# A hybrid decoder block on one core: mixers of two blocks taken together, w_in of the second pair as seven block products, the second MLP product accumulated over all of K

## The chip, the core and the metric

The kernel runs on one core of a Trainium2 chip. The metric is device time in microseconds of one execution; lower is better. The engines named here: PE (TensorE, matmuls), ACT (ScalarE), DVE (VectorE), POOL (GpSimd), SP (SyncE, which issues DMAs).

## What is computed

One layer on x of 2048 rows and 1024 columns, in float32. Cut to what matters:

```python
h = rmsnorm(x, norm_mix_g)
u = h @ w_in                                  # 1024 x 3584
gate_b, gate_c, v, x_r, g = split(u)          # 512, 512, 512, 1024, 1024
y_conv = gate_b * causal_dwconv(gate_c * v, conv_w)
xr = causal_dwconv(x_r, rnn_conv_w) + rnn_conv_b
y_rnn = rg_lru(xr, w_a, b_a, w_x, b_x, lru_lambda) * gelu(g)
y = concat[rmsnorm(y_conv), rmsnorm(y_rnn)]
x = x + y @ w_out                             # 1536 x 1024
z = square(relu(rmsnorm(x, norm_mlp_g) @ w_mlp_in))   # 1024 x 4096
x = x + z @ w_mlp_out                         # 4096 x 1024
out = rmsnorm(x, final_norm_g)
```

`rg_lru` takes two gates r and i from block-diagonal products of xr, forms a = exp(-8 r softplus(-lambda)) and runs the recurrence s = a s + sqrt(1 - a^2) i xr along the rows.

## The kernel before

The 2048 rows are four blocks of 512 (`TB`). Every product is made in three passes: an operand is split into a rounded part (`_hi`, a cast on ACT, L153) and the rest (`_lo`, a subtraction on DVE, L154), and PE multiplies hi by hi, hi by lo and lo by hi. Names ending in these are the two parts.

Blocks are taken in pairs. For a pair b, b + 1 the order is: `mixers(b)` (L933), `w_out_rows(b)` (L958) and `w_out_conv(b)` (L980), `mixers(b + 1)`, `w_out_rows(b + 1)`, `w_out_conv(b + 1)`, then the MLP of both blocks.

- `mixers`: w_in in 14 units of 256 columns, 48 matmuls of 512 columns each (`mm_cols`, L193; tiles ps_x, ps_g, ps_c, ps_v, ps_b). Each weight is loaded and split again for every block. Four units of x_r and g feed four steps of the recurrence (`lru_conv`, `lru_gelu`, `lru_scan`; two channel tiles of 512 rows each; psri are the gate products, L584, and L610 is the scan). Units c, v and b then make the short convolution.
- `w_out_rows` and `w_out_conv` split y (`split_y`, L500 on ACT and L501 on DVE: y_hi, y_lo), multiply by w_out (po, L213), add to x (L970, L993), normalize (L338, tiles xs), and transpose on PE (tps, L976; copied on ACT by L978).
- The first MLP product, `Up` (L675), takes the two blocks as a 2 x 2 block product in seven products (Winograd's form): the operands H1 to H7 are sums of the two blocks' h, the weights sums of four quarters of a slice of w_mlp_in, 8 slices x 7 x 24 matmuls (up, L731). z goes to DRAM (d_z).
- The second, `Down` (L787), does the same with w_mlp_out: four slices `s` of K, in each seven products over two parts `a`, 24 matmuls each (dn, L845); after each product of each slice the sum in PSUM is added to x on DVE (`drain`, L857): 112 additions in all. The weight sums (L815 to L822) are made again for each pair.
- `finish` normalizes the rows and stores them (L874).

What sets the order: inside `manual_schedule` (L400 for the start, L1081 for the MLP, PE only) the instructions stand as written. Elsewhere a scheduler sets the order of each engine's instructions; engines take them strictly in that order, and so does SP's queue of DMAs. Pools of fixed size set how far ahead a load or a split can run (`TSLOTS`, `WSLOTS`).

Of the kernel before, what the change touches and what calls it, by code (L numbers as in the profile page):

```python
# [27 lines left out]
TSLOTS = 29  # L28
WSLOTS = 15
WARM = 6  # L30
AHEAD = 2
# [3 lines left out]
LEAD2 = 2  # L35
ORDER = (1, 2, 6, 5, 7, 3, 4)

ROWS = [
    ("conv_w", 12),
# [11 lines left out]
def block_kernel(  # L51
# [3 lines left out]
    norm_mix_g,  # L55
    w_in,
    conv_w,
    rnn_conv_w,
    rnn_conv_b,
    w_a,  # L60
    b_a,
    w_x,
    b_x,
    lru_lambda,
    g_norm_conv,
    g_norm_rnn,
# [5 lines left out]
    x_t,  # L72
    out,
# [14 lines left out]
    xp = ctx.enter_context(tc.tile_pool(name="xp", bufs=2))  # L88
# [11 lines left out]
    def wtile(name, shape, dt=F32):  # L100
        return wp.tile(list(shape), dt, tag="w", name=name)
# [4 lines left out]
    def wide(name, extra):  # L106
        return xp.tile([P, 2, TB + extra], F32, tag="x", name=name)
# [3 lines left out]


    def src_col(w, col):
        v = w[:, col : col + 256].rearrange("(k p) c -> p k c", p=P)
        return [v[:, 0:4, :], v[:, 4:8, :]], (P, 4, 256)

    def src_row(w, row):
        v = w[row : row + 256, :].rearrange("(j p) n -> p j n", p=P)
        return [v[:, 0:1, :], v[:, 1:2, :]], (P, 1, D)

    def src_quad(w, row):
        v = w[row : row + 512, :].rearrange("(h j p) n -> p h j n", p=P, j=2)
        return [
            v[:, i, :, 512 * c : 512 * c + 512] for i in range(2) for c in range(2)
        ], (P, 2, 512)

    units = []
    for b in range(NB):
        for pr in range(4):
            units.append(("x%d" % pr, src_col(w_in, COL_X + 256 * pr)))  # L130
            units.append(("g%d" % pr, src_col(w_in, COL_G + 256 * pr)))
        for pr in range(2):
            for nm, col in (("c", COL_C), ("v", COL_V), ("b", COL_B)):
                units.append((nm + str(pr), src_col(w_in, col + 256 * pr)))
        for pr in range(4):
            units.append(("oB%d" % pr, src_row(w_out, 512 + 256 * pr)))
        for pr in range(2):
            units.append(("oA%d" % pr, src_row(w_out, 256 * pr)))

    raws = {}  # L140
    splits = {}
    cursor = [0]

    def load_tiles(srcs, shape, name, new):
        tiles = []
        for s in srcs:
            r = new(name, shape)
            nc.sync.dma_start(r, s)
            tiles.append(r)
        return tiles  # L150
# [1069 lines left out]
```

## Time and profile before

| | |
|---|---|
| median of 3 runs | 2210.51 us (2209.82 to 2211.15) |
| span of the profiled execution | 2208.7 us |
| mean granted PE clock | 0.994 |
| matmuls start at full rate at | 28.95 us |
| first pair: mixers and w_out until | 494 us |
| its first MLP product until | 808 us |
| its second MLP product until | 1113 us |
| second pair, last matmul at about | 2183 us |

The profiled execution is one of its own, 1.8 us below the median of the runs; its span is the only time that the profile gives for it. Views used below: the page, the chain of waits, groups of instructions by shape (busy us, mean ns of one, idle time ahead of them and what ended it), windows of time (width, busy us of PE, PEld, DVE, ACT and POOL, granted clock, DMA share, GB/s).

### The profile page before, as it was taken

To read this page: it belongs to the slowest core of one execution; us is meant where nothing else is said; L and a number is where in the kernel's file an instruction comes from. 1 tells how busy PE (TensorE), PEld (TensorE's weight loads), DVE (VectorE), ACT (ScalarE), POOL (GpSimd) and SP (SyncE) were. 2 spreads that over 40 slices of the span, in tenths; PEclk is the share of its full clock that TensorE was granted. 3 is DMA by queue.
4 is the path that set the end of the run, shared out by engine and by line. 5 is a ranking of instruction groups with operands and counts; after the bars stand their busy time and mean duration, and the time that the engine had idled before them with its cause. 6 is when DMAs were issued, how large, how long until landed. Compare 5 with 4: busy or idle time off the path is not lost.

```text
span 2208.7 us, 25232 instructions
## 1 busy us (share of the span) xinstructions
PE 2172.8 (98%) x9684; PEld 1799.6 (81%) x9684; DVE 1670.0 (76%) x1948; ACT 1038.2 (47%) x1346; POOL 62.0 (3%) x62
## 2 busy tenths in 40 slices
PE   7999999999999999999999999999999999999997
PEld 6888888887888888888888888888888888788886
DVE  7787677868775778868888776886796665887867
ACT  4864378534332334334568644764443332433343
POOL 3010000000000000000100000010000000000000
PEclk8999999999999999999999999999999999999999
DMA  7334443432444378454162434233334345854432
GB/s 223 103 123 153 140 155 115 144 116 94 162 152 163 131 254 314 141 177 145 51 234 88 157 120 172 77 115 144 124 114 178 127 166 199 301 207 158 133 103 76
DMA packets 180776, 334.10 MB, mean 151 GB/s; under 512 B 14672, under 2 KB 106928, under 8 KB 180656
## 3 DMA queue, kind: packets, MB, share of 16 engines
q1 hardware_dynamic: 180656, 332.49, 44.0%
q8 instruction: 76, 1.25, 0.2%
q14 instruction: 44, 0.36, 0.1%
HBM read 252.76 MB, written 79.69 MB: 151 GB/s over the span
## 4 chain that ended last, share of the span: by engine, by line
PE 93%; DVE 4%; DMA 1%; SPq 1%; issue 0%; ACT 0%; DVEq 0%
PE dn L845 27%; PE up L731 25%; PE po L213 11%; PE ps_g L193 8%; PE ps_x L193 7%; PE ps_b L193 4%; PE ps_c L193 4%; PE ps_v L193 4%; PE psri L584 2%; DVE H L154 1%; PE start_x L420 1%; PE tps L976 1%; DVE w_lo L154 1%; DVE x L889 0%; DMA z<-d_z 0%
## 5 line engine op out<-in xcount | busy, mean ns | idle before, releaser
L731 PE MATMUL up<-H,w_hi 128*128 128x512 f32 x1792 | 553.7, 390 | 2.6 <-ACT w_hi L153 1.9
L731 PEld LDWEIGHTS up<-H,w_hi 128*128 128x128 f32 x1792 | 336.7, 188 | 73.3 <-ACT w_hi L153 2.7
L731 PE MATMUL up<-H,w_lo 128*128 128x512 f32 x896 | 350.0, 391 | 3.2 <-DVE w_lo L154 3.2
L845 PE MATMUL dn<-w_lo,z_hi 128*128 128x512 f32 x896 | 348.9, 389 | 1.9 <-DVE w_lo L154 1.9
L845 PE MATMUL dn<-w_hi,z_hi 128*128 128x512 f32 x896 | 348.8, 389 | 0.0
L845 PE MATMUL dn<-w_hi,z_lo 128*128 128x512 f32 x896 | 348.8, 389 | 0.0
L153 ACT CAST w_hi<-w 128x1024 fp32r<-128x1024 f32 x156 | 164.1, 1052 | 346.0 <-PE up L731 164.8
L154 DVE TENSOR_TENSOR w_lo<-w,w_hi 128x1024 fp32r<-128x1024 f32 x156 | 190.3, 1221 | 119.6 <-PE up L731 43.1
L154 DVE TENSOR_TENSOR w_lo<-raw,w_hi 128x1024 fp32r<-128x1024 f32 x156 | 191.4, 1230 | 99.1 <-ACT w_hi L153 45.4
L153 ACT CAST w_hi<-raw 128x1024 fp32r<-128x1024 f32 x160 | 165.5, 1046 | 103.0 <-PE po L213 67.1
L153 ACT CAST z_hi<-z 128x1024 fp32r<-128x1024 f32 x112 | 117.7, 1051 | 198.8 <-PE dn L845 158.2
L731 PEld LDWEIGHTS up<-H,w_lo 128*128 128x128 f32 x896 | 168.6, 188 | 40.0 <-DVE w_lo L154 4.9
L845 PEld LDWEIGHTS dn<-w_lo,z_hi 128*128 128x128 f32 x896 | 168.2, 188 | 37.5 <-DVE w_lo L154 2.4
L845 PEld LDWEIGHTS dn<-w_hi,z_hi 128*128 128x128 f32 x896 | 168.2, 188 | 34.8
L845 PEld LDWEIGHTS dn<-w_hi,z_lo 128*128 128x128 f32 x896 | 168.2, 188 | 34.7
L154 DVE TENSOR_TENSOR z_lo<-z,z_hi 128x1024 fp32r<-128x1024 f32 x112 | 138.3, 1235 | 56.2 <-issue 26.5
L857 DVE TENSOR_TENSOR x<-dn,x 128x1024 f32<-128x1024 f32 x112 | 136.4, 1219 | 20.9 <-PE dn L845 20.7
L213 PE MATMUL po<-w_hi,y_hi 128*128 128x512 f32 x384 | 119.5, 392 | 0.0
L213 PE MATMUL po<-w_hi,y_lo 128*128 128x512 f32 x384 | 118.4, 389 | 0.0
L213 PE MATMUL po<-w_lo,y_hi 128*128 128x512 f32 x384 | 118.3, 389 | 0.0
L193 PE MATMUL ps_g<-h_hi,w_hi 128*128 128x512 f32 x256 | 99.8, 390 | 0.0
L193 PE MATMUL ps_g<-h_lo,w_hi 128*128 128x512 f32 x256 | 99.7, 389 | 0.0
(222 smaller groups left out, 3569.5 us busy)
## 6 DMA issues: line engine op xcount, KB each, us to landing
raw<-in_w_in_dram SPq DMA_DIRECT2D x112, 512.0 KB, 3.7
z<-d_z SPq DMA_DIRECT2D x112, 512.0 KB, 3.9
w<-in_w_mlp_in_dram SPq DMA_DIRECT2D x64, 512.0 KB, 5.8
d_z<-snap SPq DMA_DIRECT2D x64, 512.0 KB, 3.4
raw<-in_w_out_dram SPq DMA_DIRECT2D x48, 512.0 KB, 3.7
d_z<-z SPq DMA_DIRECT2D x48, 512.0 KB, 4.0
w<-in_w_mlp_out_dram SPq DMA_DIRECT2D x48, 512.0 KB, 3.6
x<-in_x_dram SPq DMA_DIRECT2D x20, 512.0 KB, 8.8
```

The costliest lines, as they stand in the source:

```text
L153: nc.scalar.copy(hi, src)
L154: (lo_engine or V).tensor_tensor(lo, src, hi.bitcast(F32), SUB)
L193: nc.tensor.matmul(ps[:, j, lo:hi], ws[k // 4][:, k % 4, j * P : (j + 1) * P], hs[:, k, lo:hi], start=k == 0 and i == 0, stop=k == KD - 1 ...
L213: nc.tensor.matmul(ps[:, half, :], ys[:, j, t * P : (t + 1) * P], ws[j][:, 0, half * 512 : (half + 1) * 512], start=first and i == 0, stop ...
L420: nc.tensor.matmul(start_x[:, j, 256 * th : 256 * th + 256], w[a][q][:, k, j * P : (j + 1) * P], h[b][:, 4 * q + k, 256 * th : 256 * th + ...
L584: nc.tensor.matmul(pr_[:, half, :], ws[:, c, :], xsrc[:, j, :], start=i == 0, stop=i == len(pl) - 1,)
L731: nc.tensor.matmul(ps[:, j, :], ws[:, k, j * P : (j + 1) * P], hs(k), start=i in (1, 2, 5) and k == 0 and n == 0, stop=k == 3 and n == len ...
L845: nc.tensor.matmul(ps[t // 2][:, t % 2, :], zs[:, p, t * P : (t + 1) * P], ws[:, p, :], start=i in (1, 2, 5) and a == 0 and p == 0 and n == 0,
L857: V.tensor_add(xt[b, th, dh], ps[th], xt[b, th, dh])
L976: nc.tensor.transpose(ps[:, k, :], xs[:, k // 4, k % 4 * P : (k % 4 + 1) * P], ident)
```

## The change

1. **Mixers by pair.** For the first pair, `mixers_plain` runs both blocks through each unit of w_in, so a weight is loaded and split once for two blocks (`both`). Block 1's h is prepared in `prepare_second` right at the start. From the kept weights it also forms the sums that seven block products need and stores them in DRAM (`keep_sums`). For the second pair, `mixers_blocks` takes w_in as seven groups of two units, each a 2 x 2 block product in seven products of 24 matmuls, with the operands H1 to H7 made from the two blocks' h during the last products of `Down` (`Operands`). A group's products stand on PE in the order 1, 2, 6, 5, 7, 3, 4; weights are fetched four products ahead and split two ahead (`FETCHW`, `LEADW`).
2. **The recurrence in units of 1024 rows.** Class `Lru` handles one channel tile over both blocks. Gelu comes from ACT's table (`Gelu_apprx_tanh`) instead of a tanh and four steps. y of the recurrence goes to DRAM and comes back for w_out. The parameters and gate weights are laid out ahead of the call (`_lay_out`).
3. **w_out** of the two blocks follows one after the other. The transposes of a row tile come two tiles later instead of one.
4. **`Down`** runs K over all 8 parts for one product before it is added to x: 28 additions instead of 112. The weight sums of w_mlp_out are made once, in the first pair (`w2_sums`, during the first 16 products), stored by POOL's queue, and read again.
5. `TSLOTS` goes from 29 to 23, `AHEAD` from 2 to 1, the pool `xp` from 2 to 4 buffers of 1024 rows; splits that POOL made are made by DVE.

The core of the diff:

```diff
-TSLOTS = 29
+TSLOTS = 23
-AHEAD = 2
+AHEAD = 1
+FETCH2 = 4
+FETCHW = 4
+LEADW = 2
...
+    def prepare_second():
+        rows = Rows(1, small("rs_x"))
+        for n in range(4):
+            rows.part(n)
+        load_xt(1)
+        rows.factors()
+        bc = temp("bcs", (P, TB))
+        rows.spread(bc)
+        for q in range(4):
+            r = xtt[1, q]
+            scale_rows(r, 2 * q, bc, 2)
+            hi, lo = split_new(r, temp, "h1")
...
+    def mixers_blocks(H, more):
+        G = [InLru(n) for n in range(4)] + [InConv(n) for n in (4, 5)] + [InGate(6)]
+        seq = [(n, i) for n in range(2) for i in ORDER[:2]]
+        seq += [(n, i) for n in range(2) for i in ORDER[2:]]
+        seq += [(n, i) for n in range(2, NG) for i in ORDER]
+        for n in range(-FETCHW, len(seq)):
+            m = n + FETCHW
+            if m < len(seq):
+                G[seq[m][0]].fetch(seq[m][1])
+            m = n + LEADW
+            if 0 <= m < len(seq):
+                G[seq[m][0]].prepare(seq[m][1])
+            if n < 0:
+                continue
+            s, i = seq[n]
+            G[s].multiply(i, H)
+            G[s].drain(i)
+            more(n)
+            if 1 <= s <= 4:
+                p = G[s - 1]
+                if i == 6:
+                    p.units[0].gate(p.gw)
+                    p.units[1].conv(p.xin)
+                    p.units[0].scan()
+                    y, acc = p.units[0].out(p.g, acc)
+                if i == 7:
+                    p.units[1].gate(p.gw)
+                    p.units[1].scan()
+                    y, acc = p.units[1].out(p.g, acc)
...
+    def w2_sums(a):
+        t = dict(zip((12, 22, 11, 21), quad("w2", (P, 2, TB))))
+        for nm in (12, 22, 11, 21):
+            load(t[nm], v[nm])
+        tt(b22, b22, b12, SUB)
+        tt(b12, b12, b11, SUB)
+        tt(b11, b11, b22, ADD)
+        tt(b21, b21, b11, SUB)
+        for i, t in ((7, b22), (5, b12), (6, b11), (4, b21)):
+            W2[a, i] = spill("w2", t, nc.gpsimd)
...
-                            stop=a == 1 and p == 1 and n == len(pl) - 1,
+                            stop=a == NS - 1 and p == 1 and n == len(pl) - 1,
...
-        ysA, ysB, accA, rB = mixers(b, h)
+        if b == 0:
+            us, ysB, accA, rB, fetched = mixers_plain(h)
+        else:
+            with tc.manual_schedule(engines={nc.tensor.engine}):
+                us, ysB, accA, rB, fetched = mixers_blocks(ops.H, finish_operands)
```

How instructions moved, at three places. First, in the second pair's mixers, on ACT, where product 1 of group 3 ends (in_9078 is its sum in PSUM, drained into xr_in; xr_8874 and xr_9026 are the two recurrence units of the group before; w_hi_9042 is the weight of product 2, w_hi_9074 that of product 6). The kernel now:

```order
L761 COPY xr_in_9103<-in_9078 128x2x512 [waits PE_49]
L514 ACT_TABLE_LOAD
L514 ACTIVATE xr_8874<-xr_8874 128x1024 [waits DVE_49]
L160 CAST xr_hi_9031<-xr_9026 128x1024 [waits DVE_49]
L160 CAST w_hi_9042<-wk_8931 128x1024 [waits DMAHW5_49,Activation_49]
L160 CAST w_hi_9074<-wk_8995 128x1024 [waits DMAHW6_49]
```

The corresponding place before, where ps_x of a unit is drained in the third block (w_hi are the weights of the units to come, L599 onwards of the recurrence follows later):

```order
L536 COPY xr_in_8371<-ps_x_8322 128x2x512 [waits PE_49]
L153 CAST w_hi_8392<-raw_8310 128x1024 [waits DMAHW3_49]
L153 CAST w_hi_8396<-raw_8312 128x1024 [waits DMAHW4_49,DVE_49,Activation_49]
L153 CAST xr_hi_8384<-xr_8375 128x1024 [waits DVE_49]
L535 COPY xr_in_8717<-halo_391 128x2x3 [waits Pool_49]
```

Before, the weights' casts follow the drain directly; now a table load, a square root and a cast of xr stand between. On DVE, the same place now (gi_8977 takes the square root's result, L516 is the scan, w_lo_9043 is the other part of product 2's weight):

```order
L515 TENSOR_TENSOR gi_8977<-gi_8977,xr_8874 128x1024 [waits Activation_49]
L161 TENSOR_TENSOR xr_lo_9032<-xr_9026,xr_hi_9031 128x1024 [waits PE_49,Activation_49]
L516 SCALAR_TENSOR_TENSOR xr_8874<-r_8976,state_351,gi_8977 128x1024 [waits DVE_49]
L161 TENSOR_TENSOR w_lo_9043<-wk_8931,w_hi_9042 128x1024 [waits DMAHW5_49,DMASW1_49,Activation_49]
L521 TENSOR_TENSOR gi_8977<-xr_8874,g_8616 128x1024 [waits DVE_49]
L161 TENSOR_TENSOR w_lo_9075<-wk_8995,w_hi_9074 128x1024 [waits DMAHW6_49,DVE_49,Activation_49]
```

w_lo_9043 now stands behind a product that takes the root, xr_lo and the scan.

Second, on ACT between the w_out of a pair's two blocks (xs_3086 is block b's last row tile, tps_3105 its third tile's transposes, y_hi_3161 the first operand of block b + 1's w_out). The kernel now:

```order
L322 ACTIVATE xs_3086,ss_3084<-x_2532 128x512 [waits DVE_49]
L600 ACTIVATE y_hi_3118<-u_1971,prm_88 128x512
L600 ACTIVATE y_hi_3124<-u_2218,prm_88 128x512 x2
L304 ACTIVATE rs_s_3091<-rs_a_3090 128x1 [waits DVE_49]
L1097 COPY raw0_2534<-tps_3105 128x2x128 [waits PE_49]
L1097 COPY raw0_2535<-tps_3105 128x2x128
L1097 COPY raw0_2536<-tps_3105 128x2x128
L1097 COPY raw0_2537<-tps_3105 128x2x128
L160 CAST w_hi_3150<-raw_3134 128x1024 [waits DMAHW2_49]
L600 ACTIVATE y_hi_3161<-y_2876,prm_88 128x512 x2
```

At the end of the first block's w_out before (ps_x_2136 is the next block's w_in, which needs no result of this block):

```order
L320 ACTIVATE rs_s_2085<-rs_a_2084 128x1 [waits DVE_49]
L978 COPY raw0_1840<-tps_2099 128x2x128 [waits PE_49]
L978 COPY raw0_1841<-tps_2099 128x2x128
L978 COPY raw0_1842<-tps_2099 128x2x128
L978 COPY raw0_1843<-tps_2099 128x2x128
L153 CAST w_hi_2227<-raw_2116 128x1024 [waits DMAHW2_49,PE_49]
L536 COPY xr_in_2185<-ps_x_2136 128x2x512 [waits PE_49]
L153 CAST w_hi_2231<-raw_2118 128x1024 [waits DMAHW3_49]
```

What follows the block's tail on PE was w_in of the next block, and is now w_out of the next block, whose first operand stands behind that tail.

Third, on ACT where the mixers end (u_2218 is the last conv part, which waits for the last ps_b; y_hi_2569 the first operand of w_out). The kernel now:

```order
L160 CAST w_hi_2558<-raw_2542 128x1024 [waits DMAHW5_49,DMAHW4_49,DVE_49]
L160 CAST w_hi_2562<-raw_2544 128x1024 [waits DMAHW6_49,PE_49]
L526 ACTIVATE q_2508<-u_2218 128x1024 [waits DVE_49]
L526 ACTIVATE q_2511<-u_2218 128x1024
L600 ACTIVATE y_hi_2569<-y_2273,prm_88 128x512
L600 ACTIVATE y_hi_2569<-y_2273,prm_88 128x512 [waits DMAHW7_49]
```

The same place before (cv_1444 takes the square of the last conv part):

```order
L500 ACTIVATE y_hi_1562<-s_481,prm_354 128x512 x2
L500 ACTIVATE y_hi_1634<-s_674,prm_354 128x512 x2
L500 ACTIVATE y_hi_1704<-s_866,prm_354 128x512
L153 CAST w_hi_1554<-raw_1474 128x1024 [waits DMAHW5_49,DVE_49]
L153 CAST h_hi_1570<-xT_1538 128x1024 [waits DMAHW7_49,DVE_49,PE_49]
L153 CAST w_hi_1558<-raw_1476 128x1024 [waits DMAHW6_49,PE_49]
L507 ACTIVATE cv_1444<-u_1448 128x2x512 [waits DVE_49]
```

y_hi of the recurrence stood ahead of that square, and now stands behind it.

More of the change, by code (lines that the diff above doesn't have):

```diff
@@ L135, in block_kernel @@
[L135 to L138, printed above, removed]
+            units.append(("oA%d" % pr, rows_of(w_out, 256 * pr), (P, 1, D), None))
     raws = {}
     splits = {}
+    kept = {}
+    rawkept = {}
     cursor = [0]
[L144 to L150, printed above, removed]
@@ L157, in load_unit, with split_unit @@
         if u < len(units) and u not in raws and u not in splits:
-            raws[u] = load_tiles(*units[u][1], "raw", wtile)
-    def split_unit(u, lo_engine=None):
+            nm, srcs, shape, _ = units[u]
+            tiles = []
+            for s in srcs:
+                r = wtile("raw", shape)
+                load(r, s)
+                tiles.append(r)
+            raws[u] = tiles
+    def split_unit(u):
         if u >= len(units) or u in splits:
@@ L163, in split_unit, with take @@
         load_unit(u)
[L164 to L174 removed]
+        rs = raws.pop(u)
+        n = units[u][3]
+        if n is not None:
+            rawkept.setdefault(n, []).extend(rs)
+        splits[u] = tuple(zip(*[split_new(r, wtile, "w") for r in rs]))
+    def take(nm, ahead=AHEAD):
         u = cursor[0]
@@ new lines, in add_sq, with load_gate, new_xin @@
+    def add_sq(acc, y, q):
+        nc.scalar.activation(q, y, AF.Square)
+        if acc is None:
+            return q
+        V.tensor_add(acc, acc, q)
+        return acc
+    def load_gate(pr):
+        raw = gp.tile([P, 2, 2, P], F32, name="gate_raw")
+        nc.gpsimd.dma_start(raw, gate_w[:, 2 * pr : 2 * pr + 2])
+        t = temp("gate", (P, 2, 2, 2, P), F32R)
+        s = (t[:, 0], t[:, 1])
+        round_off(s[0], raw, s[1])
+        return s
+    def new_xin(pr):
+        xin = wide("xr_in", 3)
+        nc.scalar.copy(xin[:, :, 0:3], halo[:, 2 * pr : 2 * pr + 2, :])
+        return xin
@@ new lines, in conv_out, with stats @@
+    def conv_out(u, acc):
+        for j in range(2):
+            acc = add_sq(acc, u[:, j, :], temp("q", (P, 2 * TB)))
+        return acc
+    def stats(acc, n, nm):
+        res = []
+        for blk in range(2):
+            ps = psum("sps", (P, NT))
+            for t in range(NT):
+                a = blk * TB + t * P
+                nc.tensor.matmul(
+                    ps[:, t : t + 1], acc[:, a : a + P], ones[:, 0:1], start=True, stop=True
+                )
+            ss = small("ys_" + nm)
+            V.tensor_scalar(ss, ps, float(D) / n, None, MUL)
+            r = small("yr_" + nm)
+            rstd_of(r, ss, NT)
+            res.append(r)
+        return res
@@ L1086, in block_kernel @@
             seq += [(s, i) for s in range(3, NS) for i in ORDER]
-            downs = [Down(s) for s in range(NS // 2)]
+            down = Down(b)
+            dseq = [(i, a) for i in ORDER for a in range(NS)]
             for n in range(-LEAD1, len(seq)):
```

1238 lines of the change are left out of this document (642 added, 596 removed).

## The prediction

> **What bounds the kernel now.** I read the page's busy times first, then the chain of waits, then what PE (TensorE) waited for. PE's two lines of the page:
>
> ```profile
> PE 2172.8 (98%) x9684; PEld 1799.6 (81%) x9684; DVE 1670.0 (76%) x1948; ACT 1038.2 (47%) x1346; POOL 62.0 (3%) x62
> PE 93%; DVE 4%; DMA 1%; SPq 1%; issue 0%; ACT 0%; DVEq 0%
> ```
>
> PE is the path in every stage; DVE (VectorE), at 76%, is next. Four pieces of the chain (start us, us, what) give the price of a matmul, and show that PE goes from one stage into the next without a break:
>
> ```profile
> 47.69 10.88 PE ps_x L193 x48
> ...
> 179.92 11.05 PE ps_b L193 x48
> 190.97 43.52 PE po L213 x192
> ...
> 259.02 0.87 PE tps L976 x8
> 259.89 10.90 PE ps_x L193 x48
> ...
> 808.66 304.64 PE dn L845 x1344
> ```
>
> A 512-wide matmul takes 10.88/48 = 0.2267 us in w_in, 304.64/1344 = 0.2267 in the second MLP product. At 190.97 w_out starts the moment ps_b ends; at 259.89 the next block's w_in starts the moment the transposes of the block before end. Any wait put into these joints shows fully. Two stages show how near DVE stands to PE (busy us of PE, PEld, DVE, ACT, POOL; then the granted clock):
>
> ```profile
> 37.00:190.00 153.00, 153.00 (x679) 126.47 (x678) 129.27 (x170) 105.20 (x134) 15.64 (x13) 1.00 0.43 141
> ...
> 808.00:1113.00 305.00, 305.00 (x1347) 252.61 (x1347) 250.44 (x242) 124.27 (x140) 6.72 (x4) 1.00 0.51 172
> ```
>
> DVE is at 84% in the mixers and 82% in the second MLP product, and PE is busy through all of both. So freeing DVE there gains nothing; only matmuls or PE waits count. One place in the middle of the run shows what waits do to the clock:
>
> ```profile
> 530.00:531.00 1.00, 0.55 (x3) 0.13 (x1) 1.00 (x2) 0.58 (x1) 0.00 (x0) 1.00 0.00 0
> 531.00:532.00 1.00, 0.49 (x2) 0.30 (x2) 1.00 (x2) 0.46 (x1) 0.00 (x0) 1.00 0.00 0
> 532.00:533.00 1.00, 0.25 (x2) 0.00 (x0) 1.00 (x2) 0.00 (x0) 0.00 (x0) 1.00 0.00 0
> 533.00:534.00 1.00, 0.79 (x3) 0.71 (x4) 1.00 (x2) 0.81 (x1) 0.00 (x0) 0.91 0.00 0
> 534.00:535.00 1.00, 1.00 (x3) 0.73 (x3) 0.97 (x2) 0.24 (x1) 0.00 (x0) 0.50 0.00 0
> ...
> 537.00:538.00 1.00, 1.00 (x5) 0.78 (x5) 0.00 (x0) 0.00 (x0) 0.00 (x0) 0.89 0.69 274
> ```
>
> After four microseconds in which PE was busy 2.08, the clock is 0.50 until about 537.2, some 3.4 us: a loss of 1.7 us behind the wait itself.
>
> **The change, part by part.** The span is 2208.7; the median of the runs is 1.8 above it, and I add that at the end.
>
> *Matmuls.* Counted in the programs, the 512-wide matmuls of w_in go from 2640 to 1296 plain ones and 1176 in seven block products (7 groups x 7 x 24): 168 fewer. MLP, w_out and gate products keep their counts. 168 x 0.2267 = **-38.1 us**. DVE's drains of the second MLP product go from 112 to 28, 84 x 1.2 = 100 us of DVE, and its weight sums from 64 to 32; by the second window above DVE is not the bound there, so I cost this at 0. What it can give back at most is what dn ever waited for DVE (us in total, times, longest):
>
> ```profile
> PE dn L845 <- DVE w_lo L154: 1.9, 1, 1.9
> ```
>
> That is its low end.
>
> *Second pair's mixers.* The groups' products follow each other on PE in written order; product 2 follows product 1 with nothing between. The rows of order in the part on the change show that on ACT (ScalarE) product 2's w_hi stands behind the drain of product 1, a table load, a square root and xr_hi; and that on DVE its w_lo stands behind gi, xr_lo and a scan. Durations (us busy, mean ns of one):
>
> ```profile
> L153 ACT CAST w_hi<-raw 128x1024 fp32r<-128x1024 f32 x160 | 165.5, 1046 | 103.0 <-PE po L213 67.1 <-PE ps_v L193 18.5 <-PE ps_b L193 7.6
> L606 ACT ACT_TABLE_LOAD x15 | 19.2, 1283 | 0.3
> L606 ACT ACTIVATE v<-v 128x1024 f32<-128x1024 f32 x16 | 17.0, 1062 | 3.6 <-DVE v L605 3.5
> L536 ACT COPY xr_in<-ps_x 128x1024 f32<-128x1024 f32 x15 | 15.1, 1007 | 18.0 <-PE ps_x L193 18.0
> L153 ACT CAST xr_hi<-xr 128x1024 fp32r<-128x1024 f32 x16 | 16.9, 1054 | 66.6 <-DVE xr L550 66.6
> ```
>
> ```profile
> L154 DVE TENSOR_TENSOR w_lo<-raw,w_hi 128x1024 fp32r<-128x1024 f32 x156 | 191.4, 1230 | 99.1 <-ACT w_hi L153 45.4 <-PE ps_v L193 16.8 <-PE ps_x L193 8.4
> L610 DVE TENSOR_TENSOR_SCAN v<-r,state,gi 128x512 f32<-128x512 f32 x32 | 39.3, 1268 | 0.1
> L607 DVE TENSOR_TENSOR gi<-gi,v 128x1024 f32<-128x1024 f32 x16 | 19.5, 1217 | 0.0
> L154 DVE TENSOR_TENSOR xr_lo<-xr,xr_hi 128x1024 fp32r<-128x1024 f32 x16 | 19.6, 1222 | 0.0
> ```
>
> From the end of product 1, ACT: 1.0 + 1.3 + 1.05 + 1.0 + 1.05, less 0.1 at each change, is 5.2 us to w_hi. DVE: the root is there at 3.4, gi to 4.6, xr_lo to 5.8, the scan of 1024 (two of 512, less the overlap: 2.35, an estimate) to 8.1, w_lo to 9.2. PE has two matmuls that need no w_lo (0.45): it waits 8.7 us. Three groups (in the order numbers 2, 3 and 4) have this order: 26.1. Group 5 has w_lo behind conv, gi, scan and y: 5.6 by the same rows. I find none in groups 0, 1 and 6. Sum **+31.7** (low: w_hi alone, 3 x 5.2 = 15.6; high: DVE, whose six or seven conv steps in the row before each w_lo may be late too, 11 each, 44). In the kernel before, ACT has the next w_hi right behind the drain of xr_in.
>
> *Mixers into w_out, twice.* Before, y_hi of the recurrent part was ready long ahead: the mixers of one block ended with the conv part, and the timeline of ACT shows y_hi (four of them) running ahead of the last drain, at 190.97:
>
> ```profile
> 185.77 2.55 ACT L500 ACTIVATE y_hi<-s,prm 128x512 fp32r<-128x512 f32 x4
> ...
> 192.69 1.06 ACT L507 ACTIVATE cv<-u 128x1024 f32<-128x1024 f32 x1
> ```
>
> Now the two squares of the last u stand ahead of the first y_hi on ACT. From PE's end: the product with ps_b on DVE 1.2, two squares 2 x 0.95, y_hi 0.7, part of y_lo 0.5: 4.3, so **+8.6** for two (low 1.9 each, without the squares; high 6).
>
> *Between the two blocks' w_out, twice.* Before, the next block's w_in, which needs nothing of this block, followed. Now w_out of block b+1 follows at once, and its first y_hi stands on ACT behind the whole tail of block b:
>
> ```profile
> L338 ACT ACTIVATE xs<-x 128x512 f32<-128x512 f32 x32 | 20.2, 632 | 40.7 <-DVE x L993 40.7
> L500 ACT ACTIVATE y_hi<-u,prm 128x512 fp32r<-128x512 f32 x16 | 10.8, 716 | 0.0
> L978 ACT COPY raw<-tps 128x256 f32<-128x256 f32 x32 | 9.4, 382 | 0.0
> L993 DVE SCALAR_TENSOR_TENSOR x<-po,yr_A,x 128x512 f32<-128x512 f32 x32 | 22.9, 746 | 13.4 <-PE po L213 13.2
> ```
>
> From the end of po: the add 0.7, two squares 1.4 with four y_hi between them 2.5, the square root of a column and its DVE steps 0.5, four copies 1.2, one w_hi 1.0, y_hi 0.7: 8.0, and y_lo's first half makes it 8.9. PE's two sets of transposes fill 1.74. I take 7.2 each, **+14.4** (low 3.9 without copies, w_hi and the y_hi between; high 9).
>
> *Start.* Block 1's h is now needed one product after block 0's start. Its diag and bc come behind ps_g (48 matmuls), then:
>
> ```profile
> L378 DVE SCALAR_TENSOR_TENSOR xT<-xT,gmix,bcs 128x512 f32<-128x512 f32 x24 | 18.6, 797 | 0.0
> L920 ACT COPY bcs<-bc 128x512 f32<-128x512 f32 x3 | 1.7, 582 | 3.0 <-PE bc L370 3.0
> ```
>
> Copy 0.6, two scalings 1.6, hi 1.05, lo 1.2, and the second tile's scaling paces k = 2, 3: 1.5. PE waits 5.9; with table loads in the first chain +0.7, less nothing for the removed transposes: **+6.6** (3 to 8). *First MLP product's start.* The second block's h sums now come in two units more, behind the same rows; before, this stretch lost 5.05 us of 66:
>
> ```profile
> 494.00:560.00 66.00, 60.95 (x263) 48.58 (x262) 53.59 (x69) 28.19 (x43) 0.00 (x0) 0.97 0.30 103
> ```
>
> I take **+2** over that (-1 to 4). Gelu through its table takes DVE steps off the mixers, and 1024-wide units save single issues, but by the rows above a recurrent group still holds some 42 to 46 us of DVE work (an estimate) beside 192 x 0.2267 = 43.5 of PE: 0, with a high end of 2.5 in each of four groups.
>
> *The clock.* Nine waits of 4 us and more are added. By the 3.4 us at 0.50 above each of the seven long ones (start, two between blocks, four groups) loses 1.7: **+11.9** (0 to 15.3 for nine). The Trainium skill (TensorE: Matmul & The Clock Gate, Part 1, on what is actually happening) says that PE falls to half rate after at least one idle window of about 3.4 us. By that rule a wait of 4.3 us covers a whole window in about a quarter of its positions only, an estimate from that page, and the two joints would then cost 0.9 more in all. The trace is harsher: it fell with PE busy 2.08 of 4.
>
> Sum: -38.1 + 31.7 + 8.6 + 14.4 + 6.6 + 2.0 + 11.9 = **+37.1**. 2208.7 + 37.1 + 1.8 = **2247.6**.
>
> **Rivals.**
>
> *The waits are shorter than the matmuls saved (not slower).* One mechanism: DVE gets through its scan and conv steps before product 1 ends, so that product 2 waits for w_hi alone. Then 15.6 in the groups, low ends elsewhere (3.8 + 7.8 + 3 - 1), no clock loss: -38.1 + 29.2 = -8.9, **2201.6**. It decides at 38.1 us of waits in all. For it: DVE and ACT are only at 84% and 69% in the mixers above, so slack exists. Against it: the rows that stand ahead of w_lo wait for ACT's root, which stands behind the drain of product 1, so that slack can't be used ahead of time. If nearly all were hidden, 2179.
>
> *About equal.* The waits at two thirds of mine (42) and the clock staying up: -38.1 + 42 = +4, **2214**. For it: the walk adds single durations, and neighbouring steps overlap a little.
>
> *First MLP-down stage bound by transfers.* The W2 sums are computed once, stored and read again:
>
> ```profile
> 830.00:860.00 30.00, 30.00 (x134) 24.83 (x133) 22.19 (x19) 14.87 (x15) 0.00 (x0) 1.00 1.03 402
> ```
>
> This row shows all 16 DMA engines full at 402 GB/s. Where five quads of W2 interleave with z and w, 34 tiles of 0.524 MB have to move within some 38 us: 17.8 MB at 402 is 44.3 us, **+6.3**, so **2254**. SP issues in order, and a quad's load that waits for the stores of the quad two before holds up z behind it. Against it: four products (21.8 us) of lead. The Trainium skill (DMA: Bandwidth & Descriptors, Specifications) gives 435 GB/s as the ceiling of the SBUF side; by it the stretch would take 41 us and the sum 3 less than this rival.
>
> *It doesn't do what it says.* The 168 matmuls are gone from the program by count; only their price could differ, and 0.2267 holds in every stage.
>
> **How the numbers follow.** Forecast (waits about as walked, 2216 to 2270, the transfer rival's times in it) 0.65; beyond that 0.05; waits shorter, below 2206, 0.22; about equal, 2206 to 2215, 0.08. A measurement of this kernel tells about 0.2% (4.4 us) from no change. So faster 0.22, same 0.08, slower 0.70. The range goes from the low ends of all waits, 2200, to 2270, which is the high ends of the groups and of the clock (12.3 + 3.4) and the transfers (6.3) on top of the forecast; all high ends at once (2290) are left out.
>
> **What would show it.** Right: PE's busy time at about 2147 (2172.8 - 38.1, and 12 of slow clock); PE's waits with in<-w_hi and in<-w_lo on top (about 30 us in four groups), po<-y_hi and po<-y_lo (about 23), ps_x<-h1 at about 49; granted clock 0.50 behind each. Wrong: if product 2 waits under 3 us; if the waits for y_hi are under 2; if z<-d_z becomes PE's main releaser near the first dn; or if the clock stays at 1.00 through the long waits.

## The result, and the profile after

The changed kernel takes **2273.5 us** (median of 4 runs, 2272.3 to 2275.7), the kernel before 2210.8 beside it: a ratio of 1.0286 with a 95% interval of 1.0272 to 1.0301. Slower, as forecast, but by 62.7 us and not by 37; the time lies 3.5 us above the upper end of the range.

The head of the page, PE's busy time, and the mean granted clock (0.994 before):

```profile
span 2270.5 us, 24706 instructions
...
PE 2165.8 (95%) x9514; PEld 1785.4 (79%) x9514; DVE 1505.4 (66%) x1726; ACT 973.6 (43%) x1222; POOL 75.5 (3%) x106
```

```profile
core 0: 2270.5 us, clock 0.973
```

170 matmuls fewer (168 of them 512 wide), yet PE is busy only 7 us less: 2165.8 - (2172.8 - 38.1) = 31.1 us of its busy time is the same work at a slower clock. DVE lost 165 us of work, and the kernel is slower all the same.

What PE waited for, before and after (engine, tile, line, releaser: us in total, times, longest). Before, beside the row of dn that the prediction shows:

```profile
PE gps L405 <- DMA g_row<-in_norm_mix_g_dram: 6.3, 1, 6.3
PE start_x L420 <- ACT w_hi L153: 3.9, 1, 3.9
PE up L731 <- DVE w_lo L154: 3.2, 4, 1.0
PE bc L370 <- DVE diag L364: 3.0, 2, 2.8
```

After:

```profile
PE po L229 <- ACT y_hi L600: 21.1, 4, 5.6
PE in L746 <- DVE w_lo L161: 17.0, 4, 8.4
PE in L746 <- ACT w_hi L160: 16.2, 3, 5.4
PE bc L351 <- DVE diag L349: 11.5, 3, 9.6
PE dn L1023 <- DVE w_lo L161: 9.7, 3, 6.9
PE up L746 <- DVE w_lo L161: 5.2, 2, 2.6
PE ps_x L210 <- ACT h_hi L160: 3.3, 1, 3.3
```

po and in are the waits that the prediction walked. bc is mostly the first wait of the program, 9.6 us at the very start; before, gps, start_x and bc stood there with 13.2 together, and ps_g behind them begins 0.2 us earlier than before, so this wait adds nothing. dn is the one costed at nothing.

The chain of waits (start us, us, what) at product 2 of a group, the place that the rows of order showed:

```profile
1237.70 1.01 ACT xr_in L761
1238.73 1.28 ACT L514
1240.03 1.06 ACT xr L514
1241.12 1.22 DVE gi L515
1242.44 0.95 issue
1243.39 2.35 DVE xr L516
1245.74 1.13 DVE w_lo L161
1246.91 12.39 PE in L746 x46
```

It is step by step the walk of the prediction, the scan of 2.35 included. Windows behind the wait at 1485 to 1490, where w_out starts (width, busy us of PE, PEld, DVE, ACT, POOL, granted clock, DMA share, GB/s):

```profile
1486.00:1488.00 2.00, 0.00 (x0) 0.00 (x0) 2.00 (x3) 1.77 (x3) 0.00 (x0) 1.00 0.00 0
1488.00:1490.00 2.00, 0.00 (x0) 0.00 (x0) 2.00 (x3) 2.00 (x4) 0.00 (x0) 0.87 0.01 4
1490.00:1492.00 2.00, 1.94 (x4) 1.16 (x4) 1.90 (x2) 2.00 (x5) 0.00 (x0) 0.50 0.56 156
1492.00:1494.00 2.00, 1.33 (x4) 1.00 (x4) 2.00 (x5) 1.07 (x2) 0.00 (x0) 0.50 0.96 293
1494.00:1496.00 2.00, 2.00 (x7) 1.52 (x6) 2.00 (x5) 1.39 (x2) 0.00 (x0) 0.50 0.81 239
1496.00:1498.00 2.00, 2.00 (x10) 1.63 (x9) 1.39 (x3) 0.05 (x1) 0.00 (x0) 0.93 1.03 380
```

The clock falls at about 1489.5, before work starts again, and comes back at about 1496.3: 6.8 us at half rate, twice the 3.4 us that I read off the kernel before. And the windows around the wait of 6.90 us in the second MLP product, at 835 to 842:

```profile
820.00:835.00 15.00, 15.00 (x67) 12.14 (x65) 11.89 (x10) 3.85 (x4) 2.14 (x4) 1.00 1.04 412
835.00:850.00 15.00, 8.10 (x24) 6.37 (x24) 11.41 (x10) 2.00 (x2) 2.13 (x4) 0.66 1.02 411
...
870.00:900.00 30.00, 30.00 (x134) 24.82 (x134) 23.25 (x20) 10.01 (x10) 4.26 (x8) 1.00 1.04 412
```

All 16 DMA engines are full (a share of 1.02 to 1.04) at 411 to 412 GB/s.

The terms of the sum, beside what they came to. The waits are PE's waits at each place, after less before. The clock is what PE lost at half rate: in each window of 2 us, PE's busy time times one minus the granted clock, summed over the places behind a wait (30.1 us in twelve places, against 1.7 in one place of the kernel before). The tail is the time from the end of the last matmul to the end: 2257.4 to 2270.5 after, 2196.2 to 2208.7 before (not the 2183 of the table ahead).

| term | predicted | measured |
|---|---|---|
| matmuls | -38.1 | -38.1 |
| second pair's groups (8.03, 8.43, 8.43, 8.35) | +31.7 | +33.2 |
| mixers into w_out (4.93, and 4.93 + 0.67) | +8.6 | +10.5 |
| between the two blocks' w_out (2 x 5.63) | +14.4 | +11.3 |
| start (3.26 + 1.31) | +6.6 | +4.6 |
| start of the first MLP product | +2.0 | +0.5 |
| second MLP product, W2 sums (10.8 of waits, 1.9 before) | 0 | +8.9 |
| clock | +11.9 | +28.4 |
| tail | 0 | +0.6 |
| sum | +37.1 | +59.9 |

The two spans differ by 61.8; 1.9 us are in none of the rows.

### The profile page after: what moved, and what is told of

It reads as the page before. It is cut to its first block, busy times and chain, and to the rows that moved or that the text cites. A ratio compares the mean times of both kernels' runs of the same rounds, so it can differ in the third digit from the quotient of the medians.

```text
span 2270.5 us, 24706 instructions
## 1 busy us (share of the span) xinstructions
PE 2165.8 (95%) x9514; PEld 1785.4 (79%) x9514; DVE 1505.4 (66%) x1726; ACT 973.6 (43%) x1222; POOL 75.5 (3%) x106
## 4 chain that ended last, share of the span: by engine, by line
PE 51%; DVE 5%; ACT 1%; issue 1%; DVEq 0%
PE dn L1023 22%; PE up L746 13%; PE in L746 10%; PE po L229 6%; DVE xr L516 1%; DVE w_lo L161 1%; PE psri L492 1%; DVE gi L515 0%; DVE xr L479 0%; DVE H L161 0%; ACT L514 0%; ACT w_hi L160 0%; DVE gi L521 0%; DVE x L1067 0%; ACT xr L514 0%
## 5 line engine op out<-in xcount | busy, mean ns | idle before, releaser
L161 DVE TENSOR_TENSOR w_lo<-w,w_hi 128x1024 fp32r<-128x1024 f32 x208 | 253.2, 1222 | 266.4 <-ACT w_hi L160 138.0
L160 ACT CAST w_hi<-w 128x1024 fp32r<-128x1024 f32 x208 | 215.6, 1049 | 134.3 <-PE dn L1023 117.8
L746 PE MATMUL in<-H,w_hi 128*128 128x512 f32 x784 | 248.4, 399 | 16.2 <-ACT w_hi L160 16.2
L746 PEld LDWEIGHTS in<-H,w_hi 128*128 128x128 f32 x784 | 151.4, 194 | 49.0 <-ACT w_hi L160 17.5
L161 DVE TENSOR_TENSOR w_lo<-raw,w_hi 128x1024 fp32r<-128x1024 f32 x76 | 92.8, 1223 | 125.5 <-ACT w_hi L160 84.8
L746 PE MATMUL in<-H,w_lo 128*128 128x512 f32 x392 | 156.5, 399 | 17.0 <-DVE w_lo L161 17.0
L160 ACT CAST w_hi<-raw 128x1024 fp32r<-128x1024 f32 x76 | 79.8, 1051 | 187.1 <-PE po L229 109.7
L229 PE MATMUL po<-w_hi,y_hi 128*128 128x512 f32 x384 | 123.4, 403 | 21.1 <-ACT y_hi L600 21.1
L919 ACT COPY snap<-up 128x1024 f32<-128x1024 f32 x48 | 48.7, 1014 | 193.1 <-PE up L746 193.1
```

What stands on the lines that cost most here:

```text
L160: nc.scalar.copy(hi, src)
L161: V.tensor_tensor(lo, src, hi.bitcast(F32), SUB)
L229: nc.tensor.matmul(ps[:, half, :], ys[:, j, t * P : (t + 1) * P], ws[j][:, 0, half * 512 : (half + 1) * 512], start=first and i == 0, stop ...
L746: nc.tensor.matmul(ps[:, j, :], ws[:, k, j * P : (j + 1) * P], hs(k), start=i in (1, 2, 5) and k == 0 and n == 0, stop=k == 3 and n == len ...
L919: nc.scalar.copy(t, ps)
```

## The experiments

All are edits of the changed kernel and ran against the kernel before (medians of 2210.1 to 2210.7). Differences are against the 2273.5 of the changed kernel. In the code, `...` marks lines left out.

### What a wait costs behind itself

PE multiplies operands that it already has, into the half of the sum that product 2 overwrites later, while it waits for product 2's weight in groups 2 to 5.

```diff
+        def filler(count):
+            for _ in range(count):
+                nc.tensor.matmul(ps[:, 1, :], H[1][0](0)[:, :P], H[1][0](1), start=True, stop=True)
...
+        fills = {2: (20, 10), 3: (20, 10), 4: (20, 10), 5: (0, 34)}
...
+        filler(before)
...
+                    if (j, k, n) == (0, 0, 2):
+                        filler(behind)
```

> The second pair's product 2 of groups 2 to 5 gets matmuls without use ahead of it (20 before it and 10 after its first two matmuls in groups 2, 3 and 4, 34 after the first two in group 5), whose sums are overwritten; they fit into the waits of 5.4 and 3.0 us (8.35 in group 5), and no other engine's order changes. Theory A (a long wait costs its length and then slow clock): the waits stay where they end, the clock in these four places stays at 1.00, and the span falls by 2.4 + 2.4 + 2.35 + 2.85 = 10.0 us, to about 2260.5. Rival B (the slow clock is hidden behind ACT and DVE, so that only the waits count): the span stays within 2 us of 2270.5.

2264.7 us, ratio 1.0251 (1.0233 to 1.0268): 8.8 less, with a clock of 0.986. The stretch of the chain above, in windows of the changed kernel:

```profile
1240.00:1242.00 2.00, 0.00 (x0) 0.00 (x0) 1.28 (x2) 1.99 (x4) 0.00 (x0) 0.57 0.03 12
...
1248.00:1250.00 2.00, 2.00 (x6) 1.58 (x5) 1.95 (x2) 1.06 (x1) 0.55 (x1) 0.50 0.16 63
1250.00:1252.00 2.00, 2.00 (x9) 1.59 (x8) 0.40 (x1) 1.05 (x1) 0.00 (x0) 0.87 1.00 279
```

and in one window of this kernel:

```profile
1236.00:1252.00 16.00, 14.29 (x62) 11.19 (x61) 13.47 (x11) 9.17 (x9) 1.58 (x2) 1.00 0.30 100
```

The clock stays at 1.00, and the kernel is faster although PE starts product 2 no sooner behind product 1 (5.36 us, 5.35 in the changed kernel): the slow clock is a cost of its own, 2.2 us in each of the four places.

### Which engine makes product 2 late

On ACT, product 1's drain is held behind product 2's w_hi, from group 2 on.

```diff
...
+            if i == 1 and s > 1:
+                with tc.issue_after(G[s].ins[2][0].ins):
+                    G[s].drain(i)
...
```

> On ACT alone, product 1's drain of groups 2, 3 and 4 is queued behind product 2's w_hi (no change on DVE or PE). Theory A (as predicted: ACT's chain from the end of product 1 makes the wait): w_hi is ready before product 1 ends, the root and with it gi, xr_lo, scan and w_lo come up to 3.3 us earlier, and PE's waits in these groups fall from 8.4 to about 5, some 10 us in all, to about 2260. Rival B (DVE is itself late: its conv and recurrence steps run without a break until 3.3 us after product 1's end, so that the root is not what gi waits for): the wait for w_hi goes, the one for w_lo grows from 3.0 to about 8, and the span stays within 3 us of 2270.5.

2274.6, ratio 1.0292 (1.0276 to 1.0307): no change. PE's waits in this kernel:

```profile
PE in L750 <- DVE w_lo L163: 16.8, 4, 8.4
PE in L750 <- ACT w_hi L162: 15.7, 3, 5.4
```

Both stay. The square root and xr_hi still stood ahead of w_hi on ACT, and with the drain gone the root waited for DVE's step L515 of the recurrence:

```profile
1241.50 1.06 ACT L516 ACTIVATE xr<-xr 128x1024 f32<-128x1024 f32 x1 [0.83 <-DVE xr L515]
```

So ACT's chain is not the cause by itself; DVE gets there just as late. Rival B was right on the time, and wrong that the wait for w_hi would go.

Product 2's weight fetched and split two products earlier, in groups 2 to 5:

```diff
...
+            if 1 <= here[0] <= 4 and here[1] == 5:
+                G[here[0] + 1].fetch(2)
...
+            if 1 <= here[0] <= 4 and here[1] == 7:
+                G[here[0] + 1].prepare(2)
```

> In the second pair, product 2's weight of groups 2 to 5 is fetched and split two products earlier than the others, so that its w_hi and w_lo stand ahead of the recurrence's last steps on ACT and DVE. Theory A (DVE's order makes these waits: the work would fit, but w_lo stands behind steps that are late): the four waits of 8.4 us and their slow clock (10.0) mostly go, a group takes about 44 to 46 us instead of 54.7, and the span falls by 35 to 43 us, to about 2232. Rival B (DVE is full: 43.1 us of work in a group against 43.5 of PE, with dependencies that leave it idle for 11.5): the wait moves to another product of the group, a group takes 50 us or more, and the span falls by under 20 us.

2246.3, ratio 1.0167 (1.0152 to 1.0183): 27.2 less, between the 35 to 43 of A and the under 20 of B. PE's waits, and one group (54.7 us in the changed kernel) as a window:

```profile
PE in L746 <- DVE w_lo L161: 9.2, 9, 1.9
...
PE psri L492 <- DVE xr_lo L161: 2.9, 3, 1.0
```

```profile
1235.30:1283.70 48.40, 44.71 (x192) 35.82 (x192) 43.32 (x38) 39.45 (x38) 3.83 (x5) 1.00 0.34 109
```

The order made the waits: the same work, split earlier, loses 6.3 us less in each of these groups. Some 3.7 us a group stay, mostly in small waits, with DVE busy 43.3 of 48.4; at full clock, since none is long.

### w_out and the start

The first y of w_out split before the last squares of the mixers, and before the tail of the first block:

```diff
...
         fetched = [fetch_y(ysB, pr, 1) for pr in range(2)]
+        fetched[0] = split_y(fetched[0], "g_norm_rnn", 0)
...
```

> The first y_hi and y_lo of w_out are formed before the squares of the last conv part, and for a pair's second block before the tail of its first block. Theory A (what stands ahead of y_hi on ACT makes these waits, and each is followed by slow clock): the waits of 4.9 and 5.6 us and their slow clock (2.9 and 2.9 in the first pair, 2.8 and 2.8 in the second) go, 21.8 + 11.4 = 33 us less, about 2237. Rival B (another operand is late at the same places, such as the second w_lo or the sums): waits of 2 us and more stay in the four places, and the span falls by under 20 us.

2245.8, ratio 1.016 (1.0145 to 1.0175): 27.7 less, of the 33 that A expected. Of po's 21.1 us of waits 3.5 are left, for the second tile:

```profile
PE po L229 <- ACT y_hi L600: 3.5, 2, 1.8
```

21.8 us of waits were there (21.1 + 0.67), and 18.3 went. The other 27.7 - 18.3 = 9.4 fit the clock: in the changed kernel 11.4 us were lost behind these four waits, and here 1.7 is left, behind the second tile's wait in one place.

Block 1's spread in the middle of ps_g:

```diff
-                wg = both("g0", drain_g, (0,))
-                prepare_second()
+                wg = take("g0")
+                drain_g(0, col_products("g0", wg, h[0], prepare_second))
...
```

> Block 1's bc comes in the middle of ps_g's 48 matmuls instead of behind them, so that its h is formed some 5.4 us earlier. Theory A (the chain behind bc makes the wait of 4.6 us at the start): wait and slow clock (2.8) go, 7.4 us less, about 2266. Rival B (ACT and DVE are busy with weights there, so that h comes no earlier): under 3 us less.

2267.0, ratio 1.0255 (1.024 to 1.027): 6.5 less. ps_x waits for nothing any more, and the clock stays up there.

### Transfers, or the order on DVE

The W2 sums are not stored, and products 4 to 7 of the second MLP product read plain quarters of w_mlp_out in their place, in both pairs; that part of the computation is left out.

```diff
-            W2[a, i] = spill("w2", t, nc.gpsimd)
+            W2[a, i] = v[{7: 22, 5: 12, 6: 11, 4: 21}[i]]
```

> The sums of W2 are still loaded and formed, but not stored (32 transfers of 0.5 MB fewer in the first pair's second MLP product), and products 4 to 7 read the quarters of W2 itself: part of the product is left out. Theory A (transfers bound this stretch): the wait of 6.9 us at its second product and the three small ones after it (3.9) mostly go, with 2.9 of slow clock, and the span falls by 9 to 13 us, to about 2259. Rival B (the wait is for DVE's place in line, the sums ahead of w_lo): the 6.9 stays, and the span falls by under 4 us.

2260.9, ratio 1.023 (1.0215 to 1.0245): 12.6 less. The windows of the same stretches now:

```profile
835.00:850.00 15.00, 13.79 (x61) 11.08 (x60) 11.96 (x11) 8.75 (x9) 0.00 (x0) 1.00 0.99 374
870.00:900.00 30.00, 30.00 (x134) 24.85 (x133) 25.10 (x22) 10.01 (x10) 0.00 (x0) 1.00 1.00 384
```

Still near full, but no longer late. The fourth sum made later, in products 16 to 31:

```diff
+    def w2_last(a):
+        load(b21, w2_quarters(a)[21])
+        load(b6, W2[a, 6])
+        V.tensor_tensor(b21, b21, b6, SUB)
+        W2[a, 4] = spill("w2", b21, nc.gpsimd)
...
```

> Of W2's quarters three are loaded and three sums stored during the first 16 products of the first pair's second MLP product, and the fourth sum is made during products 16 to 31 (two loads, one store): 16 transfers of 0.5 MB fewer in the first stretch, 8 more in all. Theory A (amount of transfers in the first stretch makes the waits of 6.9 + 3.9 us): the large wait falls below 4 us, and the span falls by 4 to 9 us, to about 2267. Rival B (what counts is when the first quads come, at the end of the first MLP product, not how many there are): the 6.9 stays, within 2 us of 2273.

2274.7, ratio 1.0296 (1.0279 to 1.0314): no gain. The wait of 6.9 became 4.5; four small ones came in its place, and that of bc in this stretch grew from 1.2 to 3.0. The edit takes 16 of 96 transfers out of the first 16 products; at the full rate of 411 GB/s there is room for 68 in their 87 us, so 80 are still too many.

At 837 of the changed kernel a subtraction of the W2 sums stands on DVE ahead of z and of the w_lo that PE waits for, and waits for its load:

```profile
837.29 1.23 DVE L976 TENSOR_TENSOR w<-w 128x1024 f32<-128x1024 f32 x1 [2.33 <-DMA w<-in_w_mlp_out_dram]
```

So the order on DVE was a rival. Those steps held behind the split for the product two ahead:

```diff
...
+        with tc.issue_after(last[0].ins):
+            tt(b22, b22, b12, SUB)
...
```

> The changed kernel, with the DVE steps of the W2 sums (and so their stores) held behind the split of the weight that is two products ahead, where the change lets them run ahead of the last steps of the first MLP product. The loads, the sums and the stores are the same in number. In the changed kernel's trace three subtractions of the sums (at 821, 827 and 837) stood waiting 2.3, 1.8 and 2.3 us for their loads, ahead of z and of the first w_lo on DVE. Theory A, the wait of 6.90 us comes from that order on DVE: dn<-w_lo falls under 3 us in all, and the time by 8 to 11 us with the clock, to 2262 to 2266. Theory B, the transfers' amount alone makes it (96 tiles in 87 us are 577 GB/s against 411 to 417 measured): the wait stays at 6 or more, or goes to another product of that stretch, and the time is 2270 or more.

2278.1, ratio 1.0308 (1.0294 to 1.0322): 4.5 worse. Windows of this kernel, where dn's waits of 3.42 and 2.42 now are, and PE's waits:

```profile
880.00:900.00 20.00, 16.59 (x66) 13.32 (x65) 16.16 (x16) 5.91 (x6) 3.72 (x7) 0.91 1.04 412
900.00:920.00 20.00, 17.58 (x70) 14.01 (x69) 13.89 (x14) 6.70 (x7) 2.67 (x5) 0.91 1.04 414
```

```profile
PE dn L1026 <- DVE w_lo L163: 7.8, 5, 3.4
...
PE dn L1026 <- ACT w_hi L162: 1.9, 1, 1.9
```

The first wait went, and the longest now stands 46 us later, with the DMA engines as full. In this stretch PE's waits are about as long in sum (12.2 us, 10.8 in the changed kernel), but the clock falls three times instead of once and costs 6.5 us instead of 2.9; that is most of the 4.5. The order set where the waits stand, not whether they come. The next edit moves less in the stretch: only the sums of products 6 and 4 are stored, those of 5 and 7 made where they are used, from two loads.

```diff
...
+            if i in (5, 7):
+                self.w[i, a], other = duo("w2", (P, 2, TB))
+                for t, nm in zip((self.w[i, a], other), {5: (12, 11), 7: (22, 12)}[i]):
+                    load(t, w2_quarters(a)[nm])
...
+                V.tensor_tensor(w, w, self.other.pop((i, a)), SUB)
```

> The same treatment of the W2 sums in the changed kernel without any other edit. Theory A: of the 10.8 us of waits of the second MLP product at most 3 are left and the slow clock behind the longest goes: 8 to 11 us less than 2273.5, so 2262 to 2266. Theory B: as the run that split off only the fourth sum, 2272 or more.

2266.1, ratio 1.0252 (1.0238 to 1.0266): 7.4 less, just short of A. One wait of 4.60 at the first dn is left and one of 1.06, 186 us later; between them dn does not wait at all. So with 64 transfers in place of 96 the later waits are gone or small, as the amount would have it. The first one is the wait that the order on DVE had moved in the run before; the last run below puts both edits together.

The sums moved into the first MLP product, where the DMA engines are about half busy (five of eight parts, then all; both on top of the three edits of the next part):

```diff
+                if more and n >= W2_FROM and (n - W2_FROM) % W2_STEP == 0 and (n - W2_FROM) // W2_STEP < W2_UP:
+                    w2_sums((n - W2_FROM) // W2_STEP)
...
+        if a < W2_UP:
+            t = {nm: wtile("w2") for nm in (12, 22, 11, 21)}
```

> As the run with three edits, but five of the eight parts of the W2 sums are formed during the first MLP product of the first pair (one part every six products from product 22 on, in buffers of the weights' pool), and three in the second MLP product. In the first 16 products of the second one 56 tiles of 0.524 MB have to move instead of 96: 29.4 MB in 16 x 5.45 = 87 us is 337 GB/s, under the 411 to 417 that the trace showed as full. Theory A, the amount in that stretch makes the waits there: dn's waits for w_hi and w_lo (about 10 us and 5 of slow clock in the run with all four edits) fall under 4, time 2195 to 2201 us, faster than the kernel before. Theory B, it isn't the amount but the loads' place in SP's queue or the buffers: dn's waits stay above 8, time 2207 or more. Theory C: the sums' buffers hold up the weights of the first MLP product, and up<-w_hi or up<-w_lo get over 5 us of waits.

> As the run before, but all eight parts of the W2 sums in the first MLP product, one every four products from product 20 on: 64 tiles in some 174 us there, 193 GB/s on top of about 175, and 32 tiles (192 GB/s) left in the first 16 products of the second one. Theory A: no wait of dn over 1 us, time 2193 to 2198 us. Theory C: DVE, at about 60% in the first MLP product, gets 39 us more in 174, and the sums' buffers stand in the way of the splits: new waits of up of 5 us and more, so slower than the run with five parts.

2213.0 (1.0011, 1.0002 to 1.0021) and 2223.1 (1.0062, 1.0047 to 1.0077), against 2208.2 without the move: worse, and the more so the more parts are moved. In the first, the first dn still waits 7.3 us, with no more than 56 transfers in the 16 products. That wait does not follow the amount (6.9 us with 96, 4.6 with 64, 7.3 with 56); it is gone where no sums are left to form there (the second run) and in each run that holds the sums on DVE. In the second, PE's top wait:

```profile
PE up L752 <- DVE w_lo L164: 25.0, 9, 4.8
```

dn waits for nothing any more (A was right that far), and the first MLP product pays more than that: 25.0 against 5.2. Theory C; whether DVE's 39 us or the buffers taken from the weights weigh more was not tried.

### Together

Early y, early split and start together, with and without the later fourth sum:

> The three edits on the waits together (first y parts of w_out formed early, product 2's weight of groups 2 to 5 split two products earlier, block 1's spread in the middle of ps_g), with the W2 sums where the change has them, all four in the first 16 products. Theory A, the savings of the single runs add: 2273.5 - 27.7 - 27.2 - 6.5 = 2212 us. Theory B, a stage pays back what the one before it gains (the sums' loads start earlier, so their transfers meet the second MLP product as full as before): no more than 2 us away from the run with all four edits (2209.8), on either side. Theory C, the split of the sums was what held that run up: under 2205.

> Early split of product 2, first y_hi early, block 1's bc early and W2's sums in two parts, together. Theory A in all four: 2273.5 - 27.7 (measured) - 39 - 7.4 - 6 = about 2193, 0.8% faster than the kernel before the change. Rival B for the groups alone (DVE full): about 2215, no faster than before.

2208.2 (0.9993, 0.9984 to 1.0003) and 2209.8 (0.9998, 0.9988 to 1.0007). The savings add to somewhat more than their sum (2212), and the later fourth sum adds nothing, where 2193 was forecast with it. Theory B of the first run is met as well, the two runs being 1.6 us apart; these two cannot tell it from A. Then the three edits with the second y early as well, first with the sums held on DVE, then with two sums instead of four:

> The run with three edits, with the W2 sums held on DVE as in the run beside it, and with the second y tile of w_out formed early too. Theory A: from 2208.2 the waits of the first second-MLP products (4.5 + 0.9 + 1.0 + 1.3, and 1.6 at the end of the first MLP product) and 3.3 of slow clock behind them go, and 2 x 1.76 at w_out: 2193 to 2199 us, faster than the kernel before by 0.5% or more. Theory B, transfers: 3.5 from w_out alone, 2203 to 2207.

2210.0 (0.9999, 0.999 to 1.0009): the 3.5 us of w_out went, and the second MLP product took them back: with the sums held, waits of 1.9 to 3.1 us stand in five places of it.

> The run with three edits and both first y tiles of w_out early, and of the W2 sums only those of products 6 and 4 are made once and stored (6 in the first 16 products, 4 in the next 16); those of products 5 and 7 are a difference of two quarters, made from two loads where they are needed, in both pairs. In the first 16 products 64 tiles of 0.524 MB have to move instead of 96: 33.6 MB in 87 us, 385 GB/s, under the measured 411 to 417. Nothing holds the sums behind the splits on DVE. Theory A, the amount in a stretch makes the waits: dn waits under 3 us in all, with 3.5 from w_out 2194 to 2201 us, faster than the kernel before. Theory B, the transfers are too many wherever they stand, or 385 is too near to full: 2204 or more.

**2199.5, ratio 0.9949 (0.9936 to 0.9963)**: faster than both kernels, by 74 us against the changed one. Its PE and its waits:

```profile
PE 2143.2 (97%) x9514; PEld 1768.5 (80%) x9514; DVE 1530.7 (70%) x1750; ACT 976.4 (44%) x1226; POOL 58.0 (3%) x90
```

```profile
PE in L749 <- DVE w_lo L161: 9.2, 9, 1.9
PE dn L1044 <- DVE w_lo L161: 7.7, 3, 6.4
PE up L749 <- DVE w_lo L161: 5.2, 2, 2.6
PE psri L494 <- DVE xr_lo L161: 3.4, 4, 1.0
```

With the same 9514 matmuls PE is busy 22.6 us less than in the changed kernel: that is the clock. Of the 38.1 us saved in matmuls 11 arrive; the groups' small waits (9.2 + 3.4) and the first dn (6.4) hold most of the rest.

The same with the sums held on DVE as well, for the 6.4 us that are left at the first dn:

> The run with two W2 sums instead of four and all other edits, with the sums also held on DVE behind the split for the product two ahead. Its only long wait of dn was 6.4 us at the first product, with 2.0 of slow clock about it. Theory A, that wait is the order on DVE (the subtractions wait for their loads ahead of the first w_lo) and there is now room for the transfers: it goes, and 6 to 8 us with it, 2191 to 2194. Theory B, the transfers at that place make it in any order: it comes out again some products later, 2198 or more.

2200.8, ratio 0.9958 (0.9944 to 0.9972): B. The first dn waits no more, and at 983 to 1002 five waits come, of 7.4 us together:

```profile
PE dn L1047 <- ACT w_hi L162: 4.3, 2, 3.4
...
PE dn L1047 <- DVE w_lo L163: 3.2, 3, 1.1
```

That is just behind the second 16 products (891 to 983 us), into which the fourth sum and the doubled loads of product 5 were moved. By the count of 64 transfers both stretches stand at 385 GB/s, yet the DMA engines moved 410 to 414 from 900 to 960 us. The count left something out: in the second 16 products this trace also has four loads of x and four of its transpose, and 72 transfers are more than the 68 that there is room for. Which transfer comes late there was not followed up.

## Why the prediction came out as it did

**Matmuls: right.** 168 x 0.2267 is in PE's busy time, and with the waits mostly removed part of it shows as a faster kernel.

**Second pair's groups: right in size (31.7, measured 33.2), and incomplete in cause.** The walk gave 8.7 us for w_lo and the groups show 8.03 to 8.43; group 5 waits 8.35 instead of 5.6, the one order that I took from fewer rows. I put the chain down to ACT. Holding the drain back changed nothing, since DVE's recurrence was as late; only an earlier split helped. My words against the first rival, that slack can't be used ahead of time, hold for the order as written: the rows behind the root can't run earlier, but the weight's split could.

**w_out: right.** Joints 10.5 for 8.6, between blocks 11.3 for 14.4; the chain of y_hi behind squares and tail is shown by the run that moves y_hi.

**Start and first MLP product: right place, a little over.** 4.6 for 6.6, and 0.5 for 2.

**The clock: the step that failed.** "By the 3.4 us at 0.50 above each of the seven long ones (start, two between blocks, four groups) loses 1.7: +11.9 (0 to 15.3 for nine)." It was 28.4. Of the 16.5 missed, 6.7 is the size: those seven places lost 18.6, some 2.7 each and not 1.7. The rest is places that the forecast counted at nothing: the two joints into w_out 5.6, the wait for the W2 sums 2.9, the start of the first MLP product 1.4 more than before. I took the length from one place before, where work came back just as the clock fell, so that one span of 3.4 us at half rate was all. After a wait that ends inside such a span, the rest of that span and a whole further one run at half rate: the row at 1490 shows 6.8 us. Ten places lost 2.35 to 2.92 us each, two with shorter waits, at the first MLP product, 1.4 and 1.6. A size from one event was made into a bound; nine at 1.7 as the high end was below what came. The Trainium skill (TensorE: Matmul & The Clock Gate, Part 1, on what is actually happening) says that the windows of about 3.4 us run freely, and that full rate comes back after at least one busy window. If a window in which PE only starts again does not count as busy, that gives between one and two windows of half rate behind the wait, an estimate from that page of 1.7 to 3.4 us lost; the trace agrees with 2.35 to 2.92 at the ten places. I had used that page only for when the clock falls, not for when it rises.

**W2's transfers: a rival that came true beside the forecast.** "+6.3" stood there as a case of its own; 8.9 us of waits came, and with their clock 12.6 went when the stores went. I held four products of lead against it. A lead of 22 us does not help against a shortage that lasts over 100: 96 tiles of 0.524 MB against the room for 68 in 16 products at 411 GB/s. The path was another than the rival's: not z held up in SP's queue, but a late load that a subtraction on DVE waited for, ahead of PE's w_lo (6.9 of the 10.8 us of waits). The rival belonged into the sum, since it needed nothing but the transfers' own count.

**The chances.** The case of short waits (0.22) did not come; no wait of the walk was hidden. The range had the high ends of groups, clock and transfers together, 22 us above the forecast. The clock went 13.1 us past its own high end and the transfers 2.6 past theirs. That the time still came out only 3.5 us above the range is luck: the groups used 1.5 of the 12.3 us kept for them. That 84 additions fewer on DVE gain nothing is not shown: it was not tried alone.

## What to carry to other kernels

Price a wait of PE as the wait plus the half-rate time behind it, in the changed kernel 2.4 to 2.9 us for each wait of 3.3 us and more and in the other runs 1.6 to 3.2: twelve places cost nearly as much as the waits of the four groups. Where a change saves work on the bound engine, first look in the written order for what now stands ahead of the next stage's first operand; moving three steps forward brought back all of the 63 us lost. Count all the bytes of a stretch against its length before and after the change: holding the sums only moved the shortage, and fewer transfers made it smaller here.

## What the runs showed of the hardware

- The clock falls and rises on steps of about 3.4 us: 3.4, 6.8 and, where it fell inside the wait of a group (1240.3 to 1250.5), 10.2 us at half rate. It does not need a long pause: waits of 2.6 us at the start of the first MLP product cost 1.4 and 1.6, and nothing in the run with three edits, where the same two waits stand at another place in the steps.
- What counts is how much of a step PE is busy. With steps of 3.41 us laid on the clock's changes in the traces of all 18 kernels (from 30 us on), each of the 138 steps behind which the clock fell had PE busy, as the profile has it, for 0.48 of it or less, and of the thousands behind which it stayed up none was under 0.44. At half rate, a step with PE busy for 0.82 or less was followed by another at half rate (124 times), one with 0.85 or more by full rate (138 times). So a step in which PE only starts again does not bring the clock back.
- Matmuls whose result nobody uses keep it up: 30 to 34 of them in each of four waits kept the clock at 1.00 and gained 8.8 us.
- The 16 DMA engines held 411 to 418 GB/s for over 100 us with loads and stores mixed. The Trainium skill (DMA: Bandwidth & Descriptors, Specifications) gives 435 GB/s as the ceiling on the side of SBUF; these runs stayed 4 to 6% below.
- The table load on ACT took 1.28 us, and the root behind it started 0.02 us later (1238.73 to 1240.03 in the chain above).
